# RMSNorm and matmul on one core: a load of eight tiles placed behind the stores of the first eight

## The chip, the cores and the metric

The kernel runs on one core of a Trainium2 chip. The metric is the device time of one execution in microseconds, as the median of several runs. The engines are named as in the profile: PE is the tensor engine, DVE the vector engine, ACT the scalar engine, POOL GpSimd, and SP (SyncE) the engine that issues nearly all transfers here.

## What is computed

```python
x: (16, 1024, 512) float32; gamma: (512,); weight: (512, 768) float32

rms = np.sqrt(np.mean(x ** 2, axis=-1, keepdims=True) + eps)
x_norm = x / rms * gamma
out = np.matmul(x_norm, weight)        # (16, 1024, 768) float32
```

There are 16,384 rows of x. The kernel works in 128 tiles of 128 rows: a tile of x has 262 KB, a tile of the output 393 KB. 33.6 MB of x and 1.6 MB of weights are read, and 50.3 MB are written.

## The kernel before

Tiles are handled in pairs (pair j is tiles 2j and 2j+1). For each pair GpSimd casts x to bf16, PE transposes it (two bf16 values as one float32 word) into PSUM, DVE evacuates the transposed pair, PE multiplies it with the weights (which hold gamma), and ACT and DVE scale one tile each by 1/rms on the way from PSUM to the output tile. ACT also sums the squares. The order on every engine is the order of the program.

x comes in groups of 16 tiles with two buffers, the output in groups of 8 tiles with three:

```python
XG, OG = 16, 8
AHEAD = 20
x_first, x_size = stretches(XG, {0: [2, 2, 4, 8], **{g: [8, 8] for g in (1, 4, 5, 6, 7)}})
o_first, o_size = stretches(OG, {0: [2, 2, 4], 1: [4, 4], last: [4, 4]})
...
xin = ctx.enter_context(tc.tile_pool(name="xin", bufs=2))
xbp = ctx.enter_context(tc.tile_pool(name="xb", bufs=4))
...
opsum = ctx.enter_context(tc.tile_pool(name="opsum", bufs=3, space=bass.MemoryType.PSUM))
outp = ctx.enter_context(tc.tile_pool(name="out", bufs=3))
```

So the first group is loaded in stretches of 2, 2, 4 and 8 tiles, the second in 8 and 8, the third and fourth in 16 at once. The first eight tiles are stored as 2, 2 and 4, the next eight as 4 and 4, then 8 at a time.

All loads of x and all stores are issued by SyncE, and SyncE takes its instructions in the order of the program: a store waits there until its tiles are scaled, and what stands behind it waits too.

```python
def load_until(i):
    while starts and starts[0] < i:
        load(starts.pop(0))          # one dma_start on SyncE for each stretch

def store(i):
    first, n = o_first[i], o_size[i]
    if i == first + n - 1:
        nc.sync.dma_start(out=rows(out, first, n), in_=held(o_tiles, OG, first, n))
```

Every group of 16 tiles but the first has four tiles (the last ones of the group, a quad) that PE doesn't transpose: GpSimd casts all four in one instruction, and DVE transposes them in 32x32 blocks, three instructions in each round of the loop.

```python
def cast_quad(q):
    quads[q] = quad_in.tile([P, 4, D], BF16, name="xq")
    nc.gpsimd.tensor_copy(out=quads[q], in_=held(x_tiles, XG, 4 * q, 4))
    ...

load_until(2)
load_weights(0)
load_weights(1)
load_until(2 * XG)                       # tiles 2 to 31
for _ in range(20):
    nc.sync.drain()
... # pair 0
for j in range(1, NP):
    load_until((2 * j + AHEAD + XG - 1) // XG * XG)
    if j + 3 < NP and quad_of(j + 3) is None:
        cast(2 * j + 6, nc.gpsimd, 2)
    if (2 * j + 2) % XG == 0 and 2 * j + 2 < NT:
        cast_quad((2 * j + 2 + XG - 4) // 4)
    elif 2 * j >= XG:
        move_quad(3)                     # 32x32 blocks of the quad, on DVE
    ...
    # the transposes of pair j + 2 are put between the matmuls of pair j
    for i, engine in ((2 * j, nc.scalar), (2 * j + 1, nc.vector)):
        a = accumulator()
        matmuls(i, a, range(K), feed)
        finish_tile(i, a, engine)        # scales, and stores when a stretch is full
```

`load_until` in the loop rounds up to whole groups: for j up to 6 it asks for tiles below 32, and from j = 7 for tiles below 48. `cast_quad` in round 7 casts tiles 28 to 31.

Of the kernel before, what the change touches and what calls it, by code (L numbers as in the profile page):

```python
# [18 lines left out]
def kernel(  # L19
# [18 lines left out]
    XG, OG = 16, 8  # L38
    AHEAD = 20
# [40 lines left out]
    def load(i):  # L80
        if i // XG not in x_tiles:
            x_tiles[i // XG] = xin.tile([P, XG, D], F32, name="xt")
        nc.sync.dma_start(out=held(x_tiles, XG, i, x_size[i]), in_=rows(x, i, x_size[i]))  # L83
# [3 lines left out]
    def load_until(i):  # L87
        while starts and starts[0] < i:
            load(starts.pop(0))

    def cast(i, engine, n=1):
        if i // 2 not in xb_tiles:
            xb_tiles[i // 2] = xbp.tile([P, 2, D], BF16, name="xb")
        engine.tensor_copy(out=xb_tiles[i // 2][:, i % 2:i % 2 + n, :], in_=held(x_tiles, XG, i, n))  # L94
# [13 lines left out]
    def norms(i, n):  # L108
        ssq = stats.tile([P, 4], F32, name="ssq")
        for t in range(n):  # L110
            square(i + t, ssq[:, t:t + 1])
        root(i, n, ssq)
# [30 lines left out]
    def transpose_tile(i):  # L143
        for h in range(2):
            transpose_word(i // 2, i % 2, h)
        evac(i // 2, i % 2, 1)
# [6 lines left out]
    def quad_of(j):  # L153
        return j // 2 if (2 * j) % XG >= XG - 4 and 2 * j >= XG else None
# [4 lines that stand above are left out]
        turned = quad_out.tile([P, 4, 2, P, 2], BF16, name="xTq")  # L159
        for n in range(2):  # L160
            xT_tiles[2 * q + n] = turned[:, 2 * n:2 * n + 2]
        words = quads.pop(q).rearrange("p t d -> p (t d)").bitcast(F32).rearrange("p (a w) -> p a w", w=P)
        out_words = turned.rearrange("p t h m c -> p (t h m c)").bitcast(F32).rearrange("p (a m) -> p a m", m=P)
        for tokens in range(0, P, B):
            for features in range(0, P, B):
                quad_moves.append((out_words[features:features + B, :, tokens:tokens + B],
                                   words[tokens:tokens + B, :, features:features + B]))

    def move_quad(n):
        for _ in range(min(n, len(quad_moves))):  # L170
            dst, src = quad_moves.pop(0)
            nc.vector.transpose(out=dst, in_=src)  # L172

    def scale(engine, dst, src, r):
        if engine is nc.scalar:
            nc.scalar.mul(out=dst, in_=src, mul=r)  # L176
        else:
            nc.vector.tensor_single_scalar(out=dst, in_=src, scalar=r, op=mybir.AluOpType.mult)  # L178

    def accumulator():  # L180
        return opsum.tile([P, 2, WIDE], F32, name="ops").rearrange("p a b -> p (a b)")
# [16 lines left out]
    def matmuls(i, acc, ks, feed=None):  # L198
        for k in ks:
            matmul(i, k, acc, 0, WIDE)  # L200
            if feed:
                feed()
            matmul(i, k, acc, WIDE, O)

    def finish_tile(i, acc, engine):
        scale(engine, out_tile(i), acc[:, :O], rstd_of[i])
        store(i)


    def feeder(pairs, gaps, alone=False):  # L210
        queue = [(j, t, h) for j in pairs for t in range(2) for h in range(2)]
        calls = iter(gaps)

        def feed():
            for _ in range(next(calls)):
                j, t, h = queue.pop(0)
                transpose_word(j, t, h)
                if alone and h == 1:
                    evac(j, t, 1)
                elif (t, h) == (1, 1):  # L220
                    evac(j)
        return feed

    with tc.manual_schedule():
        g_row = singles.tile([2, P, 2], F32)
        nc.scalar.dma_start(out=g_row, in_=gamma.rearrange("(h w c) -> h w c", w=P, c=2))
        nc.scalar.preload_act_table(AF.Sqrt)  # L227
        wv = weight.rearrange("(h w c) o -> w h (c o)", w=P, c=2)
        w_f32 = singles.tile([P, K, O], F32)

        def load_weights(h):
            nc.sync.dma_start(out=w_f32[:, 2 * h:2 * h + 2, :].rearrange("p c o -> p (c o)"), in_=wv[:, h, :])  # L232

        load_until(2)
        load_weights(0)
        load_weights(1)
        load_until(2 * XG)

        for _ in range(20):
            nc.sync.drain()  # L240


        warm = singles.tile([P, WIDE], BF16)
        nc.vector.memset(warm, 0.0)
        eps_sb = singles.tile([P, 1], F32)
        nc.vector.memset(eps_sb, float(eps))  # L246
        ident_f = singles.tile([P, P], F32)
        make_identity(nc, ident_f)
        spare = accumulator()

        def warm_up(n):
            for _ in range(n):
                nc.tensor.matmul(out=spare[:, :WIDE], lhsT=warm[:, :P], rhs=warm, start=True, stop=True)  # L253

        w_bf = singles.tile([P, K, O], BF16)

        def weights(k, engine, lo=0, hi=O):
            scale(engine, w_bf[:, k, lo:hi], w_f32[:, k, lo:hi], g_sb[:, k % 2, k // 2:k // 2 + 1])


        probe = singles.tile([16, 16 * 64], F32)

        def mark(counts):
            for k in counts:
                nc.sync.dma_start(out=probe[:k, 64 * k:64 * k + 4 * k], in_=x[:k, :4 * k])

        warm_up(6)
        gp = tpsum.tile([P, 2, 2], F32, name="tp")
        for c in range(2):
            nc.tensor.transpose(out=gp[:, c, :], in_=g_row[:, :, c], identity=ident_f[:2, :2])  # L270
        g_sb = singles.tile([P, 2, 2], F32)
        nc.vector.tensor_copy(out=g_sb, in_=gp)  # L272
        cast(0, nc.gpsimd)
        cast(1, nc.gpsimd)
        cast(2, nc.gpsimd, 2)
        norms(0, 2)
        warm_up(4)
        transpose_tile(0)
        transpose_tile(1)
        warm_up(2)  # L280
        weights(0, nc.vector, 0, WIDE)
        weights(0, nc.vector, WIDE, O)
        weights(1, nc.scalar)
        acc = [accumulator() for _ in range(2)]
        for i in range(2):
            matmuls(i, acc[i], [0, 1])
        weights(2, nc.vector)
        weights(3, nc.scalar)
        norms(2, 2)
        cast(4, nc.gpsimd)  # L290
        cast(5, nc.gpsimd)
        matmuls(0, acc[0], [2, 3])
        finish_tile(0, acc[0], nc.scalar)
        matmuls(1, acc[1], [2, 3], feeder([1], [2, 2], alone=True))
        finish_tile(1, acc[1], nc.vector)
        cast(6, nc.gpsimd, 2)

        mid, one, two, both = ([0, 0, 1, 1, 0, 1, 1, 0], [1, 1, 0, 1, 1, 0, 0, 0], [1, 0, 1, 0, 1, 0, 1, 0],
                               [1, 1, 1, 1, 1, 1, 1, 1])
        marks = {NP - 10: (12, 13, 14, 15)}  # L300
        for j in range(1, NP):
            load_until((2 * j + AHEAD + XG - 1) // XG * XG)
            if j + 3 < NP and quad_of(j + 3) is None:
                cast(2 * j + 6, nc.gpsimd, 2)
            if (2 * j + 2) % XG == 0 and 2 * j + 2 < NT:
                cast_quad((2 * j + 2 + XG - 4) // 4)
            elif 2 * j >= XG:
                move_quad(3)
            if j < 4:
                norms(2 * j + 2, 2)  # L310
            if 3 <= j < NP - 2:
                norms_by_four(j + 2)
            if j in marks:
                mark(marks[j])
            if j < 3:
                feed = feeder([j + 1], mid if j == 1 else one, alone=j == 1)
            elif j == 3:
                feed = feeder([4, 5], both)
            elif j + 2 < NP and quad_of(j + 2) is None:
                feed = feeder([j + 2], two)  # L320
            else:
                feed = None
# [3 lines that stand above are left out]
                finish_tile(i, a, engine)  # L326
# [35 lines left out]
```

## Time and profile before

| What | Before |
|---|---|
| time, median of 3 runs | 210.36 us (210.36 to 210.41) |
| span of the profiled execution | 209.0 us |
| granted clock of PE, mean | 0.983 of full speed |
| HBM read and written | 35.14 MB and 50.33 MB |

The profile is one execution, recorded by the hardware. Its page gives the busy time of each engine, the span in 40 slices (one digit for the busy share of an engine, numbers for GB/s), the chain of work that ended last, and groups of instructions. From the trace behind it one can ask for windows (busy time and number of instructions of PE, PE's weight loads, DVE, ACT and POOL, then granted clock, DMA share and GB/s of each stretch) and for timelines of one engine (start, duration, engine, line, what is written from what, number of instructions, and in brackets the idle time before and what ended it). A line such as L94 is a line of the kernel, which may be that of a helper: L94 is the cast of a pair, L158 the cast of a quad, L133 a transpose on PE, L140 its evacuation, L172 a 32x32 move on DVE, L194 a matmul, L176 and L178 the scaling on ACT and DVE, L83 a load of x, L191 a store.

### The profile page before, as it was taken

Reading aid. Unit: us, or ns where it says so; the run is one execution under the profiler, and the core shown is the slowest. Engines: PE = TensorE matmul, PEld = TensorE weight load, DVE = VectorE, ACT = ScalarE, POOL = GpSimd, SP = SyncE. Lnnn points to the kernel's source line nnn. Section 1 sums busy time; section 2 is a strip of 40 time slices with the busy share of each in tenths; the row PEclk is TensorE's granted clock in tenths of the full one; section 3 lists DMA queues with packets and bytes.
Section 4 is the critical chain, followed back from the end, with each engine's and each line's share of the span. In section 5 each row is a group of like instructions: output and inputs, shape, how many; then the busy total and the mean of one; then the engine's idle time right before and its main releaser. Section 6 shows DMA issues by size and latency. Waiting matters only on the chain.

```text
span 209.0 us, 3478 instructions
## 1 busy us (share of the span) xinstructions
PE 194.0 (93%) x1238; PEld 129.2 (62%) x1238; DVE 150.8 (72%) x270; ACT 149.4 (71%) x358; POOL 64.7 (31%) x65
## 2 busy tenths in 40 slices
PE   7699999999999999999999999999999999999700
PEld 2367776665677666666766667666677666666400
DVE  0465657997399957998499957998499957998300
ACT  4698787778677887788777887788777884976300
POOL 3247554003910292055210562025610365000000
PEclk9999999999999999999999999999999999999985
DMA  6999999999999999999999999999999999999991
GB/s 254 420 438 433 339 399 428 460 434 395 438 438 433 420 423 417 431 423 445 408 431 433 441 420 428 428 428 434 420 433 420 444 433 419 433 419 386 390 435 52
DMA packets 5601, 85.69 MB, mean 410 GB/s; under 512 B 718, under 2 KB 720, under 8 KB 1488
## 3 DMA queue, kind: packets, MB, share of 16 engines
q1 hardware_dynamic: 5580, 85.47, 96.9%
q8 instruction: 9, 0.15, 0.3%
q14 instruction: 8, 0.07, 0.1%
q10 hardware_dynamic: 4, 0.00, 0.0%
HBM read 35.14 MB, written 50.33 MB: 409 GB/s over the span
## 4 chain that ended last, share of the span: by engine, by line
PE 78%; DMA 14%; POOL 1%; DVE 1%; SPq 1%; issue 1%; POOLq 0%
PE ops L194 68%; DMA xt<-in_x_dram 14%; PE tp L133 9%; POOL xb L94 1%; DVE ot L178 1%; SPq L232 0%; SPq L83 0%; SPq L191 0%; POOLq L94 0%; DVE xT L140 0%
## 5 line engine op out<-in xcount | busy, mean ns | idle before, releaser
L194 PE MATMUL ops<-w_bf,xT 128*128 128x512 bf16 (+1 forms) x800 | 147.6, 326 | 0.9 <-DVE w_bf L178 0.8
L194 PEld LDWEIGHTS <-xT 128*128 128x128 bf16 x800 | 78.3, 98 | 46.8 <-issue 1.0
L176 ACT ACTIVATE ot<-ops,rstd 128x768 f32<-128x768 f32 x64 | 57.6, 901 | 41.9 <-PE ops L194 41.3
L94 POOL CAST xb<-xt 128x1024 bf16<-128x1024 f32 (+1 forms) x52 | 51.2, 1010 | 99.0 <-DMA xt<-in_x_dram 85.5
L98 ACT ACTIVATE jk<-xt 128x512 bf16<-128x512 f32 x128 | 78.8, 619 | 2.1 <-DMA xt<-in_x_dram 2.1
L178 DVE TENSOR_SCALAR ot<-ops,rstd 128x768 f32<-128x768 f32 x64 | 64.6, 1009 | 9.5 <-PE ops L194 9.0
L133 PE MATMUL tp<-ident_f,xb 128*128 128x128 f32 x200 | 54.1, 274 | 1.2 <-POOL xb L94 1.1
L140 DVE COPY xT<-tp 128x1024 bf16<-128x1024 bf16 (+1 forms) x53 | 34.6, 656 | 25.2 <-PE tp L133 24.6
L172 DVE STREAM_TRANSPOSE xTq<-xq 32x256 f32<-32x256 f32 x112 | 48.8, 435 | 1.9
L194 PE MATMUL ops<-w_bf,xTq 128*128 128x512 bf16 x224 | 42.8, 326 | 0.0
L133 PEld LDWEIGHTS tp<-ident_f,xb 128*128 128x128 f32 x200 | 27.9, 141 | 5.2 <-POOL xb L94 3.0
L194 PEld LDWEIGHTS <-xTq 128*128 128x128 bf16 x224 | 22.0, 98 | 12.3
L98 ACT ACTIVATION_READ_ACCUMULATOR jk<-xt 128x1 f32 x128 | 24.4, 191 | 0.0
L158 POOL CAST xq<-xt 128x2048 bf16<-128x2048 f32 x7 | 13.3, 1896 | 11.3 <-DMA xt<-in_x_dram 11.3
L102 ACT ACTIVATE rms<-ssq,eps_sb 128x4 f32<-128x4 f32 (+1 forms) x35 | 10.4, 297 | 1.1
L104 DVE RECIPROCAL rstd<-rms 128x4 f32<-128x4 f32 (+1 forms) x35 | 6.1, 175 | 6.3 <-ACT rms L102 5.6
L253 PE MATMUL ops<-warm 128*128 128x512 bf16 x12 | 4.4, 505 | 1.2 <-DVE eps_sb L246 1.2
L253 PEld LDWEIGHTS <-warm 128*128 128x128 bf16 x12 | 1.2, 117 | 2.6 <-DVE eps_sb L246 1.2
L176 ACT ACTIVATE w_bf<-w_f,g_sb 128x768 bf16<-128x768 f32 x2 | 1.9, 936 | 1.2 <-DMA w_f<-in_weight_dram 0.9
L272 DVE COPY g_sb<-tp 128x4 f32<-128x4 f32 x1 | 0.2, 161 | 3.2 <-PE tp L270 3.2
L227 ACT ACT_TABLE_LOAD x1 | 1.3, 1283 | 1.3 <-PEq L343 1.3
L178 DVE TENSOR_SCALAR w_bf<-w_f,g_sb 128x512 bf16<-128x512 f32 (+2 forms) x3 | 1.4, 481 | 0.6 <-DMA w_f<-in_weight_dram 0.6
(10 smaller groups left out, 1.9 us busy)
## 6 DMA issues: line engine op xcount, KB each, us to landing
out_dram<-ot SPq DMA_DIRECT2D x13, 3072.0 KB, 17.9
xt<-in_x_dram SPq DMA_DIRECT2D x11, 2048.0 KB, 18.3
xt<-in_x_dram SPq DMA_DIRECT2D x2, 4096.0 KB
out_dram<-ot SPq DMA_DIRECT2D x5, 1536.0 KB, 11.0
w_f<-in_weight_dram SPq DMA_DIRECT2D x2, 768.0 KB, 5.0
out_dram<-ot SPq DMA_DIRECT2D x2, 768.0 KB, 16.8
xt<-in_x_dram SPq DMA_DIRECT2D x2, 512.0 KB, 3.6
xt<-in_x_dram SPq DMA_DIRECT2D x1, 1024.0 KB
```

What stands on the lines that cost most here:

```text
L94: engine.tensor_copy(out=xb_tiles[i // 2][:, i % 2:i % 2 + n, :], in_=held(x_tiles, XG, i, n))
L98: nc.scalar.activation(out=jk, in_=held(x_tiles, XG, i)[:, 0, :], func=AF.Square, accum_out=ssq)
L102: nc.scalar.activation(out=rms[:, :n], in_=ssq[:, :n], func=AF.Sqrt, scale=1.0 / D, bias=eps_sb)
L104: nc.vector.reciprocal(out=rstd[:, :n], in_=rms[:, :n])
L133: nc.tensor.transpose(out=tp_tiles[j][:, t, h, :], in_=words[:, lo:lo + P], identity=ident_f)
L140: nc.vector.tensor_copy(out=dst[:, t:t + n, :], in_=src[:, t:t + n, :])
L158: nc.gpsimd.tensor_copy(out=quads[q], in_=held(x_tiles, XG, 4 * q, 4))
L172: nc.vector.transpose(out=dst, in_=src)
L176: nc.scalar.mul(out=dst, in_=src, mul=r)
L178: nc.vector.tensor_single_scalar(out=dst, in_=src, scalar=r, op=mybir.AluOpType.mult)
L194: nc.tensor.matmul(out=acc[:, lo:hi], lhsT=xT_tiles[i // 2][:, i % 2, k // 2, :, k % 2], rhs=w_bf[:, k, lo:hi], start=(k == 0), stop=(k == ...
L253: nc.tensor.matmul(out=spare[:, :WIDE], lhsT=warm[:, :P], rhs=warm, start=True, stop=True)
```

## The change

Tiles 24 to 31 are no longer loaded at the start, ahead of all stores. Their load is issued in round 4 of the loop, so on SyncE it stands behind the stores of tiles 0 to 7. It is meant to let the first stores run earlier, and to load tiles 24 to 31 nearer to their use. In round 4 `load_until` still asks for tiles below 32, and from round 7 on everything is as before.

```diff
         load_until(2)
         load_weights(0)
         load_weights(1)
-        load_until(2 * XG)
+        load_until(2 * XG - 8)
 ...
         for j in range(1, NP):
-            load_until((2 * j + AHEAD + XG - 1) // XG * XG)
+            if j >= 4:
+                load_until((2 * j + AHEAD + XG - 1) // XG * XG)
```

## The prediction

> **What bounds the kernel now.** I read the head of the page first, then the chain, then the last quarter, and then the stretch that the change touches.
>
> ```profile
> span 209.0 us, 3478 instructions
> PE 194.0 (93%) x1238; PEld 129.2 (62%) x1238; DVE 150.8 (72%) x270; ACT 149.4 (71%) x358; POOL 64.7 (31%) x65
> ...
> GB/s 254 420 438 433 339 399 428 460 434 395 438 438 433 420 423 417 431 423 445 408 431 433 441 420 428 428 428 434 420 433 420 444 433 419 433 419 386 390 435 52
> ...
> PE 78%; DMA 14%; POOL 1%; DVE 1%; SPq 1%; issue 1%; POOLq 0%
> ```
>
> Two things run nearly full: PE is busy 194.0 of 209.0 us, and the transfers move about 430 GB/s in nearly every slice. Which of them sets the end? The chain is 78% PE, and the largest other link in it is DMA. The end of the run, cut into windows (the last two columns are the DMA share and GB/s), tells which one has slack:
>
> ```profile
> 186.00:187.00 1.00, 1.00 (x9) 0.65 (x8) 0.96 (x3) 1.00 (x4) 0.00 (x0) 1.00 1.09 467
> 187.00:188.00 1.00, 1.00 (x8) 0.61 (x7) 0.97 (x2) 0.88 (x3) 0.00 (x0) 1.00 0.63 270
> 188.00:189.00 1.00, 1.00 (x8) 0.61 (x7) 0.96 (x3) 0.73 (x1) 0.00 (x0) 1.00 0.46 197
> 189.00:190.00 1.00, 1.00 (x8) 0.61 (x7) 0.95 (x4) 1.00 (x4) 0.00 (x0) 1.00 0.92 393
> ```
>
> From 187 to 189 the transfers run half empty while PE is full: the queue has nothing left and waits for PE to finish tiles 112 to 119, whose store goes out at 188.49. After it 16 tiles of output (6.3 MB, 14.6 us at 430 GB/s) remain. So the end follows PE: a microsecond lost on PE before 187 costs about a microsecond, and one of DMA alone is lost in that hole of about 1 us. Between 51.6 and 197 PE has no idle worth a name (5.00 of every 5 us, granted clock 1.00). Whatever the change does, it does before 52 us.
>
> There the page's slice at 21 to 26 us falls to 339 GB/s. In the windows:
>
> ```profile
> 22.00:23.00 1.00, 1.00 (x8) 0.75 (x7) 1.00 (x3) 0.63 (x3) 1.00 (x2) 1.00 1.05 410
> 23.00:24.00 1.00, 1.00 (x9) 0.70 (x7) 0.12 (x2) 0.95 (x2) 0.83 (x1) 1.00 1.24 360
> 24.00:25.00 1.00, 1.00 (x8) 0.66 (x7) 0.87 (x2) 1.00 (x4) 0.77 (x1) 1.00 0.90 229
> 25.00:26.00 1.00, 1.00 (x8) 0.74 (x7) 0.75 (x1) 0.17 (x2) 0.27 (x1) 1.00 0.80 197
> 26.00:27.00 1.00, 1.00 (x9) 0.69 (x8) 0.00 (x0) 0.92 (x2) 0.00 (x0) 1.00 0.80 281
> 27.00:28.00 1.00, 1.00 (x9) 0.70 (x7) 0.83 (x2) 1.00 (x3) 0.00 (x0) 1.00 0.96 403
> ```
>
> Against 430 these six windows lack 20 + 70 + 201 + 233 + 149 + 27 = 700 KB, or 1.6 us of transfer. The DMA share stays at 0.8 and above, so the queue isn't empty: the transfers in it are slow. By their order they are the load of tiles 24 to 31, the one that the change moves. The timeline of POOL (start, duration, line, count, idle before) shows what hangs on it:
>
> ```profile
> 24.23 1.04 POOL L94 CAST xb<-xt 128x1024 bf16<-128x1024 f32 x1 [0.40 <-PE tp L133]
> 28.64 1.90 POOL L158 CAST xq<-xt 128x2048 bf16<-128x2048 f32 x1 [3.36 <-DMA xt<-in_x_dram]
> 30.47 2.03 POOL L94 CAST xb<-xt 128x1024 bf16<-128x1024 f32 x2
> 33.34 1.04 POOL L94 CAST xb<-xt 128x1024 bf16<-128x1024 f32 x1 [0.84 <-PE tp L133]
> 50.52 3.01 POOL L94 CAST xb<-xt 128x1024 bf16<-128x1024 f32 x3 [16.13 <-DMA xt<-in_x_dram]
> ```
>
> The first reader of the moved load isn't tile 24 but the four-tile cast of tiles 28 to 31, which the loop asks for in round 7, ahead of the casts of pairs 11, 12 and 13. It starts at 28.64, having waited 3.36 us for the load. At 50.52 POOL gets tiles 32 to 47, and PE, which wants their transposes, has waited 0.41 us.
>
> **What the Trainium skill says.** "DMA: Bandwidth & Descriptors", section "Queues, rings and completion order": on each DMA engine a queue's descriptors are consumed in ring order. The trace agrees: the loads issued at 3.1 and 3.6 us land 13.6 and 18.0 us later, at 16.7 and 21.6, and a store issued at 12.98 takes 17.5 us to land because it stands behind them. So order of issue is order of service. The same page, "Anatomy of one DMA", says that a semaphore wait happens on the issuing sequencer and not in the DMA engines; in the trace SyncE's waits for the stores add up to 166 us, so a load behind a store is issued only when that store's tiles are done. "HBM Reference", Specifications, gives about 425 GB/s for a core that streams alone; the trace shows 420 to 440.
>
> **The change part by part.** Bytes, instructions and arithmetic stay the same; one 2.10 MB load changes its place.
>
> 1. *Ahead of the change.* Loads and weights up to tile 23 are issued as before, so PE's start and the casts up to pair 10 (24.23) stay. Cost 0.
>
> 2. *Stores 0 to 3* were issued at 12.98 and 16.1 and now are served directly after tile 23: 1.57 MB, 3.7 us, from 21.6 to 25.3. Nobody waits for them: three output tiles are there, so the first is wanted again only by tile 24. Gain 0.
>
> 3. *The issue of the load.* It follows the store of tiles 4 to 7, which goes out at 23.10 when pair 3 is done, so at about 23.5. Does the queue run dry? The first load is issued at 0.74, and 50 GB/s run in the window from 1 to 2 us and 308 in the next: some 1.3 us from issue to the first bytes. The store is then ready at 24.4, ahead of 25.3. No hole, with 0.9 us to spare. SyncE issues nothing later because of it: tiles 8 to 11 still go at 28.85.
>
> 4. *The landing of the load.* Ahead of it are now eight tiles of stores (3.15 MB) and it has itself 2.10 MB: 5.24 MB at 430 GB/s = 12.2 us after 21.6, so 33.8; POOL follows a landing after 0.2 (21.6 to 21.81). The cast of tiles 28 to 31 moves from 28.64 to about **34.0**, if the load runs at full rate, and to 35.6 if it is as slow as before.
>
> 5. *POOL behind it.* Cast 1.83 us from start to the next start (28.64 to 30.47), then 1.04 for pair 11: ready at 34.0 + 2.87 = 36.9 (before: 31.5). PE's first transpose of pair 11: evacuations follow every 3.04 us (DVE copies at 30.21, 33.24, 36.28), the one at 36.28 is pair 10's, and the next transpose on PE stands at 36.73. So 5.4 us of slack are used up nearly exactly: PE waits **about 0.2 us**; 1.7 us if the load stays slow. Pairs 12 and 13 follow 1.04 us apart while PE takes 3.04 a pair, so only one wait arises.
>
> 6. *DVE.* The 32x32 moves of tiles 28 to 31 stand in DVE's order at 34.77; now they wait for the cast's end, 34.0 + 1.9 = 35.9. DVE is 1.1 us late and can't catch up (4.8 of 5 us busy from 35 to 50). An accumulator of PE is wanted again two tiles, 3.04 us, after its own tile ends, and DVE's scaling takes 1.01 of that, so about 2 us are free, less where two tiles take only 2.6 us. The delay of 1.1 fits, barely. Cost 0, with a risk of some tenths.
>
> 7. *The load of tiles 32 to 47* has the same bytes ahead of it as before. It lands when it did (50.4), or up to 1.6 us earlier if the slow patch goes away; then PE's wait of 0.41 us vanishes. That is all that PE can win here.
>
> Sum, load at full rate: +0.2 - 0.4 = **-0.2 us**. Sum, load slow as before: +1.7, of which the wait at 51 us absorbs 0.4: **+1.3 us**.
>
> **Rivals.** (a) *Transfer bound:* the queue works better in the new order and the whole 1.6 us come off the end. The rates near 430 speak for it; against it, the dry queue at 187 to 189, where PE is the slower one. It would make 208.8. (b) *The cast takes over as the bound:* the load lands later than I sum, DVE and POOL both hold up PE, and two stalls add: the 5.4 us of slack have no reserve, each further microsecond of landing is a microsecond of stall. It would make 212 to 213. (c) *All hidden:* the slack holds and the wait at 51 us isn't there in executions without the slow patch: 210.4.
>
> **Range and chances.** Is the slow patch tied to this load's place, or to the moment? Loads of the same shape just before it run at 420 to 450 GB/s, so nothing in its form makes it slow; I give 60% that it doesn't come back. Then the time is 209.9 to 210.6, else 211 to 212. Weighted: 210.36 + 0.6 x (-0.2) + 0.4 x 1.3 = 210.8; the middle of the weight lies a little lower, so 210.6, with a range of 209.7 to 212.2. Two per cent are 4.2 us: to be faster by so much PE would have to lose idle time that it hasn't got; to be slower needs a load landing at about 39. Chances: 0.01, 0.95, 0.04.
>
> **What would show it.** Right: SyncE issues a load between the stores at 23.1 and 28.85; POOL's four-tile cast starts near 34 and names DMA as its releaser; the first stores land near 25; PE shows a short wait for POOL near 37 and none near 51; the end's hole at 187 to 189 is still there. Wrong: a cast that starts past 36, DVE waiting for POOL for more than 1.5 us with PE behind it, a queue that runs dry near 25 (step 3 has only 0.9 us), or another order of PE and DVE later on.

## The result and the profile after

The changed kernel takes 213.67 us (213.57 to 215.07, 6 runs), the kernel before 210.63 us in the same comparison (210.36 to 211.19, 6 runs). The ratio is 1.0154 with a 95% interval of 1.0125 to 1.0183: some 3.2 us slower, outside the predicted range of 209.7 to 212.2.

The page of the changed kernel (span, GB/s in 40 slices of 5.3 us, and the chain by engine):

```profile
span 211.9 us, 3454 instructions
...
GB/s 243 427 447 343 397 434 411 458 402 303 445 351 405 382 413 436 421 432 442 430 419 430 439 427 422 424 427 432 442 436 404 441 425 432 427 423 316 391 429 169
...
PE 82%; issue 8%; DMA 3%; POOL 2%; SPq 1%; DVE 0%; POOLq 0%
```

The weak slice is still there, one place sooner: 343 GB/s in the fourth slice (16 to 21 us) where the kernel before had 339 in the fifth. In windows (the last two columns are the DMA share and GB/s):

```profile
18.00:20.00 2.00, 2.00 (x16) 1.59 (x15) 1.50 (x3) 1.97 (x8) 2.00 (x3) 1.00 1.16 352
20.00:22.00 2.00, 1.95 (x15) 1.48 (x15) 0.95 (x2) 2.00 (x6) 0.91 (x1) 1.00 0.78 227
22.00:24.00 2.00, 2.00 (x14) 1.45 (x14) 1.12 (x3) 1.59 (x5) 0.97 (x1) 1.00 0.96 398
```

Against 430 they lack 156 + 406 + 64 = 626 KB, or 1.5 us. The slow stretch was 1.6 us before. But now it sits on the load of tiles 16 to 23: the load ahead of the first stores, whichever that is. It hits early work too: that load lands 19.2 us after its issue at 3.7, at 22.9 instead of 21.6.

POOL's timeline of the changed kernel shows what this made of the moved load:

```profile
23.03 3.01 POOL L94 CAST xb<-xt 128x1024 bf16<-128x1024 f32 x3 [2.12 <-PE ops L194]
37.35 1.89 POOL L158 CAST xq<-xt 128x2048 bf16<-128x2048 f32 x1 [11.31 <-DMA xt<-in_x_dram]
39.19 3.01 POOL L94 CAST xb<-xt 128x1024 bf16<-128x1024 f32 x3
50.70 3.01 POOL L94 CAST xb<-xt 128x1024 bf16<-128x1024 f32 x3 [8.50 <-PE tp L133]
```

The four-tile cast starts at 37.35 and not at 34.0, and pair 11 is ready at 40.2. PE's timeline (the bracket is idle time before, and what ended it):

```profile
36.08 0.81 PE L194 MATMUL ops<-w_bf,xT 128*128 128x256 bf16 x4
40.28 0.33 PE L133 MATMUL tp<-ident_f,xb 128*128 128x128 f32 x1 [3.40 <-POOL xb L94]
...
41.10 0.27 PE L133 MATMUL tp<-ident_f,xb 128*128 128x128 f32 x1
...
42.34 0.42 PE L133 MATMUL tp<-ident_f,xb 128*128 128x128 f32 x1
...
43.83 0.42 PE L133 MATMUL tp<-ident_f,xb 128*128 128x128 f32 x1
...
45.06 0.27 PE L133 MATMUL tp<-ident_f,xb 128*128 128x128 f32 x1
```

PE waits 3.40 us, and then there is a second loss that no wait shows. The transposes, 0.76 us apart otherwise, come 1.24, 1.49 and 1.23 us apart: 1.68 us more. In the windows from 42 to 44 the granted clock (the column ahead of the DMA share) is 0.50:

```profile
42.00:43.00 1.00, 1.00 (x5) 0.60 (x4) 0.95 (x3) 0.84 (x2) 0.20 (x1) 0.50 0.76 328
43.00:44.00 1.00, 1.00 (x4) 0.54 (x3) 0.67 (x2) 1.00 (x4) 0.00 (x0) 0.50 0.76 328
```

The kernel before has no wait near 37 us, but one of 0.41 us at 51 us, and SyncE issues a store at 82.40:

```profile
51.61 0.33 PE L133 MATMUL tp<-ident_f,xb 128*128 128x128 f32 x1 [0.41 <-POOL xb L94]
...
82.40 12.75 SPq L191 DMA_DIRECT2D out_dram<-ot  x2
```

The same store in the changed kernel:

```profile
87.06 12.75 SPq L191 DMA_DIRECT2D out_dram<-ot  x2
```

Sum on PE: 3.40 + 1.68, less the 0.41 of the old wait, which is gone: 4.67 us. The store goes out 4.66 us later. So PE's delay is accounted for, and it lasts unchanged to the last store (198.5 before, 203.1 after). But the spans differ by 2.9 us only: the end swallows some of it.

### The profile page after: what moved, and what is told of

Its sections match the earlier page's. It is cut to its first block, busy times and chain, and to the rows that moved or that the text cites. A ratio compares the mean times of both kernels' runs of the same rounds, so it can differ in the third digit from the quotient of the medians.

```text
span 211.9 us, 3454 instructions
## 1 busy us (share of the span) xinstructions
PE 195.5 (92%) x1214; PEld 130.7 (62%) x1238; DVE 151.1 (71%) x270; ACT 149.4 (71%) x358; POOL 64.7 (31%) x65
## 4 chain that ended last, share of the span: by engine, by line
PE 82%; issue 8%; DMA 3%; POOL 2%; SPq 1%; DVE 0%; POOLq 0%
PE ops L194 72%; PE tp L133 10%; DMA xt<-in_x_dram 3%; POOL xb L94 2%; DVE ot L178 0%; SPq L232 0%; SPq L83 0%; POOL xq L158 0%; POOLq L94 0%
## 5 line engine op out<-in xcount | busy, mean ns | idle before, releaser
L194 PE MATMUL ops<-w_bf,xT 128*128 128x256 bf16 (+1 forms) x783 | 148.2, 327 | 1.1 <-DVE w_bf L178 0.3
L194 PE MATMUL ops<-w_bf,xTq 128*128 128x256 bf16 (+1 forms) x217 | 42.4, 324 | 0.4
L133 PEld LDWEIGHTS tp<-ident_f,xb 128*128 128x128 f32 x200 | 28.6, 143 | 7.7 <-POOL xb L94 4.9
L158 POOL CAST xq<-xt 128x2048 bf16<-128x2048 f32 x7 | 13.3, 1895 | 19.2 <-DMA xt<-in_x_dram 19.2
L253 PE MATMUL ops<-warm 128*128 128x512 bf16 x12 | 5.5, 612 | 1.2 <-DVE eps_sb L246 1.2
```

Of the source, the lines that this page charges most:

```text
L133: nc.tensor.transpose(out=tp_tiles[j][:, t, h, :], in_=words[:, lo:lo + P], identity=ident_f)
L194: nc.tensor.matmul(out=acc[:, lo:hi], lhsT=xT_tiles[i // 2][:, i % 2, k // 2, :, k % 2], rhs=w_bf[:, k, lo:hi], start=(k == 0), stop=(k == ...
```

## The experiments

**Is it the order on GpSimd, or the order of the transfers?** First the transfers stay as in the changed kernel and the cast moves:

```diff
-            if (2 * j + 2) % XG == 0 and 2 * j + 2 < NT:
+            if j == 9:               # behind the casts of pairs 11 and 12
+                cast_quad(7)
+            elif j == 7:
+                pass
+            elif (2 * j + 2) % XG == 0 and 2 * j + 2 < NT:
                 cast_quad((2 * j + 2 + XG - 4) // 4)
             elif 2 * j >= XG:
-                move_quad(3)
+                move_quad(4 if j < 14 else 3)
```

> The changed kernel with one thing else: GpSimd casts tiles 28 to 31 in round 9, behind the casts of pairs 11 and 12, instead of in round 7 ahead of them, and DVE moves four blocks in a round instead of three. All transfers keep their order. Theory 1 (the late load holds the four-tile cast, GpSimd's order holds pair 11, PE starves for 3.4 us and then runs at a reduced clock): pair 11 is cast near 26, pair 12 near 37.4 to 38.4 and wanted at 39.8, PE's wait near 37 falls from 3.4 us to under 0.5 and the time to 210.4 to 211.2. Theory 2 (the new order of the transfers costs the time by itself, in slow stretches and in DMA engines that drift apart): the transfers are the same, so 213 to 214.

Measured: 210.70 us, ratio to before 1.0002 (0.9993 to 1.0011). The load comes about as late as in the changed kernel, but now it holds up only what needs it. POOL's timeline of this run:

```profile
36.94 1.04 POOL L94 CAST xb<-xt 128x1024 bf16<-128x1024 f32 x1 [8.83 <-DMA xt<-in_x_dram]
37.93 1.90 POOL L158 CAST xq<-xt 128x2048 bf16<-128x2048 f32 x1
```

Pair 12's cast waits for the load and still is in time; PE has no wait near 37. It has one of 1.72 us at 52.5, because DVE, with four moves a round, is behind with the quad; the granted clock stays at 1.00 after it. Counted from the first store, the store near 83 us is 1.3 us later than in the kernel before (70.68 us against 69.42), and at the end nothing of it is left. Theory 2 falls: the new order of the transfers costs no time by itself.

**The same loss without any change of transfers.** To the kernel before, matmuls of zeros are added ahead of tile 18, in an accumulator that the tile then overwrites. No work of the kernel is left out.

```diff
 a = accumulator()
+if i == 18:
+    for _ in range(24):          # 8 in the smaller run
+        nc.tensor.matmul(out=a[:, :WIDE], lhsT=warm[:, :P], rhs=warm, start=True, stop=True)
```

> The kernel before, all transfers in their old order, with 24 matmuls of zeros ahead of tile 18: PE is late by 24 x 0.215 = 5.2 us, less the 0.4 of its old wait at 51 us, so the stores of the middle are late by about 4.7, as in the changed kernel (4.66). If PE's delay alone makes the loss: 213.3 to 214.0, as the changed kernel. If the new order of the transfers has a part in it: nearer to 212 or below.

Measured: 213.88 us, ratio 1.0156 (1.0137 to 1.0175), against 1.0154 for the changed kernel. PE's delay suffices for the whole loss. The smaller dose:

> The kernel before with 8 matmuls of zeros (128x512, 0.22 us each, 1.7 us) ahead of tile 18: PE is late by 1.7 us from there on, with no idle time and no transfer changed. If the end follows PE one to one, as the prediction had it: 212.1. If one DMA engine that lags behind the others sets the end (after 204 us only 49 to 111 GB/s run in the kernel before), so that the end had some 1.7 us of slack against PE (4.66 us of delay at the last store, 2.9 at the end of the changed kernel): 210.4 to 210.8.

Measured: 210.92 us, ratio 1.0013 (0.9999 to 1.0027). Counted from the first store of each run, the store near 82 us is 1.2 us late (70.63 us against 69.42), and the end only 0.3: the prediction's sentence that a microsecond lost on PE costs about a microsecond fails here.

**How much of it is the clock?** In the changed kernel 16 such matmuls fill the time in which PE would wait.

> The changed kernel with 16 matmuls of zeros (128x512) put ahead of tile 18, so that PE works through the time in which it would wait for pair 11. If the drop of the granted clock to 0.66 between 40 and 45 us comes from PE's idle time and costs 1.3 us as I work out (4.66 us of delay in the stores at 82 us, less 3.4 us of wait, with 0.4 us of an old wait gone: 1.3 to 1.7), the clock stays at 1.00 and the stores of the middle move forward by 1.3 to 1.7 us; time 212.2 to 213, by how much of it the end takes over. If the clock falls for another reason, or costs nothing, 213.5 to 214.

Measured: 212.55 us, ratio 1.0093 (1.0069 to 1.0117), 1.1 us faster than the changed kernel. PE is never idle there, and the clock stays up, as the window after the filled wait shows:

```profile
40.00:45.00 5.00, 5.00 (x34) 3.55 (x34) 4.85 (x9) 2.79 (x7) 1.95 (x2) 1.00 0.99 426
```

Counted from the first store of each run, the store near 85 us is 1.5 us earlier than in the changed kernel (72.59 against 74.07), near the 1.68 us read off PE's timeline. So about a third of PE's delay is not the wait but the slow clock that follows it. The Trainium skill, "TensorE: Matmul & The Clock Gate" (Part 1: The HAM clock gate) says that the clock goes to half after an idle window of about 3.4 us; these runs agree as far as they go: 3.40 us idle brought 0.50, 1.72 us didn't.

**How far back may the load stand?**

```diff
-if j >= 4:
+if j >= 2:                       # behind the stores of tiles 0 to 3 only
     load_until(...)
```

> The load of tiles 24 to 31 behind the stores of tiles 0 to 3 only (round 2 instead of 4): 1.57 MB fewer ahead of it, 3.7 us. Theory 1: the cast of tiles 28 to 31 starts at 37.35 - 3.7 = 33.7, and the slack of pair 11 (36.7 - 2.9 = 33.8) just holds: PE's wait under 0.5 us, time 210.3 to 211.0. Theory 2 (putting a load behind stores costs by itself): 212 or more.

Measured: 210.89 us, ratio 1.0010 (1.0002 to 1.0019). POOL's four-tile cast:

```profile
33.33 1.90 POOL L158 CAST xq<-xt 128x2048 bf16<-128x2048 f32 x1 [7.64 <-DMA xt<-in_x_dram]
```

4.0 us sooner than behind eight tiles, and PE waits nowhere near 37. That fits the slack worked out in the prediction (a cast start at 33.8). Next, only the half of the load that nobody wants early moves:

```diff
-{0: [2, 2, 4, 8], **{g: [8, 8] for g in (1, 4, 5, 6, 7)}}
+{0: [2, 2, 4, 8], 1: [8, 4, 4], **{g: [8, 8] for g in (4, 5, 6, 7)}}
 ...
 load_until(2 * XG - 8)
+late = starts.pop(0)             # tiles 24 to 27: later, behind the stores
+load_until(2 * XG)               # tiles 28 to 31
+starts.insert(0, late)
```

> Tiles 28 to 31 are loaded ahead of all stores again, in a load of their own, and only tiles 24 to 27 behind the stores of tiles 0 to 7. Theory 1: the four-tile cast isn't late (near 25 to 27), pair 12 is wanted only at 39.8 and its load lands near 37 or sooner, so no wait of PE over 0.5 us; time 210.2 to 211. Theory 2: 213 or more, since a load still stands behind the stores and the slow stretch ahead of the first stores is still there.

Measured: 210.88 us, ratio 0.9999 (0.9988 to 1.0010). The quad's cast starts at 26.34, the cast of tiles 24 and 25 at 36.20, and PE waits for neither. It doesn't even have its old wait at 51 us, and the time is that of before: the 0.4 us that the prediction counted as the gain is worth nothing that shows at the end.

**What sets the end?** The hole at 187 to 189 us was read as a sign that the end follows PE. It can be filled:

```diff
-o_first, o_size = stretches(OG, {0: [2, 2, 4], 1: [4, 4], last: [4, 4]})
+o_first, o_size = stretches(OG, {0: [2, 2, 4], 1: [4, 4], last - 1: [4, 4], last: [4, 4]})
```

> The kernel before with the store of tiles 112 to 119 in two halves, so that the first half is issued some 5 us sooner and fills the hole at 187 to 189 us. If PE and the hole set the end: 1 to 1.7 us less, 208.7 to 209.4. If one lagging DMA engine sets it, which has no hole: within 0.4 us of before.

Measured: 210.78 us, ratio 1.0001 (0.9991 to 1.0011). The hole is gone (412 and 406 GB/s from 186 to 190), and the bulk of the transfers ends 1 us sooner. But a trickle follows it. Windows of this run:

```profile
203.00:204.00 1.00, 0.00 (x0) 0.00 (x0) 0.00 (x0) 0.00 (x0) 0.00 (x0) 0.50 0.30 123
204.00:205.00 1.00, 0.00 (x0) 0.00 (x0) 0.00 (x0) 0.00 (x0) 0.00 (x0) 0.50 0.14 61
206.00:207.00 1.00, 0.00 (x0) 0.00 (x0) 0.00 (x0) 0.00 (x0) 0.00 (x0) 0.50 0.12 49
```

and of the kernel before:

```profile
204.00:205.00 1.00, 0.00 (x0) 0.00 (x0) 0.00 (x0) 0.00 (x0) 0.00 (x0) 0.50 0.27 111
206.00:207.00 1.00, 0.00 (x0) 0.00 (x0) 0.00 (x0) 0.00 (x0) 0.00 (x0) 0.50 0.12 49
```

A full queue moves 430 GB/s with 16 DMA engines, 27 each, so 49 is, by this estimate, two engines that still work while fourteen have nothing left. The trace bears it out. It keeps 16 updates of the semaphore for each load of x and each store, taken here as one for each DMA engine's share. Of the last store before, fourteen shares land from 204.46 to 205.71, and two at 206.92 and 207.89. With the split store fourteen land by 205.00, and two at 207.52 and 207.57. So the end is that of the slowest DMA engines, and PE has some slack against them. From the runs: 1.2 us of delay of PE cost 0.3 (8 matmuls), 1.3 cost nothing (the cast moved), 3.2 cost 2.0 (the filled wait), 4.5 cost 3.3 (24 matmuls) and 4.7 cost 3.2 (the changed kernel). That is a slack of 1 to 1.5 us, and about one to one beyond it. The shares show where it goes: the first share of the changed kernel's last store lands 4.64 us later than before (209.10), as late as PE, and the last one only 2.92 us later (210.81), as the spans have it. The slowest engine is then 1.7 us behind the first, and no longer 3.4.

**Where does the slow stretch come from?** Two runs were meant to take the first stores out of the queue while tiles 24 to 31 are loaded. The first held them back in the program only:

> The kernel before with the stores of tiles 0 to 7 held back until the store of tiles 8 to 11 is issued (28.8 us), so that no store stands behind the load of tiles 24 to 31 while it runs. The slow stretch was 23 to 27 us in the kernel before, in the load of tiles 24 to 31, and 18.5 to 22 us in the changed one, in the load of tiles 16 to 23: in both the last load ahead of the first stores. If it comes from the stores that stand next in the queue, it is gone here: the load lands near 26.4 to 26.6 (21.5 + 4.9) and no window from 20 to 26 is under 400 GB/s. If it comes from the synchronous end of a long run of loads, or from the place of the data, it stays: landing near 28.5. The time itself isn't the point: the queue runs dry for some 2 us until 28.8.

Measured: 210.59 us, one run. SyncE's order of instructions came out as before, since nothing else is issued there in between: the first store went at 13.07. So it is a repeat of the kernel before, slow stretch included (246 and 296 GB/s from 24 to 28), and tells nothing of the question. The second put another store's wait ahead of them:

```diff
 if i == first + n - 1:
-    nc.sync.dma_start(out=rows(out, first, n), in_=held(o_tiles, OG, first, n))
+    held_back.insert(0, (first, n))
+    if i >= 11:                  # tiles 8 to 11 first, then 4 to 7, 2 to 3, 0 to 1
+        while held_back:
+            first, n = held_back.pop(0)
+            nc.sync.dma_start(...)
```

> The kernel before with the stores of tiles 0 to 7 issued behind the store of tiles 8 to 11, whose own wait (until 28.8 us) now stands ahead of them all: no store is in the queue while the load of tiles 24 to 31 runs. (The run named stores held was meant for this, but the order of SyncE's instructions came out as before.) If the slow stretch comes from the stores that stand next in the queue, it is gone: no window from 20 to 26 us under 400 GB/s, and the load lands at 26.4 to 26.8 instead of 28.5. If it comes from the end of the long run of loads, or from the data, it stays, and the landing is again near 28.5. The time: the queue is dry for 2 to 3 us until 28.8, in both cases; if the transfers' total counts, 211 to 213; if one lagging DMA engine sets the end and the dry stretch lets it catch up, 210 to 211.

Windows of this run, and its four-tile cast:

```profile
20.00:22.00 2.00, 1.95 (x15) 1.48 (x15) 1.02 (x2) 1.97 (x6) 1.10 (x2) 1.00 0.99 418
22.00:24.00 2.00, 2.00 (x16) 1.41 (x14) 0.99 (x3) 1.59 (x4) 1.60 (x3) 1.00 0.95 401
24.00:26.00 2.00, 2.00 (x15) 1.42 (x14) 1.30 (x2) 1.08 (x5) 0.83 (x1) 1.00 0.66 279
26.00:28.00 2.00, 2.00 (x15) 1.37 (x13) 1.28 (x2) 1.97 (x6) 0.47 (x1) 1.00 0.04 12
```

```profile
27.53 1.89 POOL L158 CAST xq<-xt 128x2048 bf16<-128x2048 f32 x1 [2.71 <-DMA xt<-in_x_dram]
```

The slow stretch is gone. From 24 us GB/s falls together with the share, since the queue runs out; before, the share stood at 0.8 to 0.9 with 197 to 281 GB/s. The cast starts 1.1 us sooner than before (28.64), less than the 1.6 summed in the prediction, because one part of the load came late (12 GB/s after 26): fifteen of the 16 shares land by 26.10 (before: 27.72), the last at 27.48 (before: 28.58). So stores that stand next in the queue slow the load ahead of them, in all 16 engines at once; by what means, no run here tells. The time of this run, 214.48 us, ratio 1.0185 (1.0168 to 1.0202), has the mechanism of the changed kernel at another place: the queue stands dry until the stores go at 28.4, the load of tiles 32 to 47 is issued at 31.61 instead of 29.28, behind all twelve tiles of stores, and PE waits 4.57 us for its casts at 55 us and then works at a clock of 0.50.

## Why the prediction was wrong

The direction of the chain was right: the moved load holds the four-tile cast, the cast holds pair 11 in GpSimd's order, and PE waits for pair 11. Steps 1 to 3 hold in what they cost: the casts of pairs 8 to 10 came up to 1.2 us later (23.03 instead of 21.81) but in time for PE, the stores of tiles 0 to 3 landed at 28.1 instead of 25.3 with nobody waiting, the load was issued at 23.48 as forecast, and the queue didn't run dry near 25 (449 GB/s from 24 to 26). Four terms were wrong.

- **Step 4, the landing: a cast start at 37.35 instead of 34.0.** "12.2 us after 21.6" had two faults. The slow stretch was counted as gone or as lying in the moved load; in fact it belongs to the load that stands ahead of the first stores, so it came back 5 us sooner, with 1.5 us. The rest, some 2 us, is a fault of the picture: a queue was treated as one pipe, with bytes divided by GB/s. What had been moved in the changed kernel from its start to 34.2 us, and to 37.35, when the cast begins:

```profile
DMA packets 1575, 13.11 MB, mean 383 GB/s; under 512 B 164, under 2 KB 166, under 8 KB 934
...
DMA packets 1696, 14.44 MB, mean 387 GB/s; under 512 B 178, under 2 KB 180, under 8 KB 948
```

  The load and everything ahead of it are 13.11 MB (7.86 up to tile 23, 3.15 of stores, 2.10 of its own). The 16 engines together had moved as much by 34.2, and yet the load is complete only at 37.3, when 14.44 MB have gone: the engines that are ahead were already 1.33 MB (3.1 us at 430 GB/s) into the next stores. In the kernel before, when tile 23 landed at 21.6, 8.34 MB had been moved for 7.86: 0.48 MB, 1.1 us. That is a spread larger by 2.0 us. The shares say who is late: of the moved load fifteen land from 34.33 to 35.16, up to 1.4 us behind the 33.8 of the prediction, and the last, alone, at 37.30. So the slow stretch, in all shares, and one late DMA engine make the 3.35 us, within the rounding. That the stores brought the spread isn't shown: a share comes late too in the run with no store in the queue (27.48). The Trainium skill, "DMA: Bandwidth & Descriptors" says (in "Two DMAs through the same engine are not ordered") that nothing orders transfers across the 16 engines; these landings agree.

- **Step 5, the wait on PE.** The slack was right but for a slip (5.2 us from 28.64 to 33.86, where the text has 5.4; the run behind four tiles shows a start at 33.33 without a wait), and with the true landing it would have given 37.35 + 2.87 - 36.73 = 3.5 us; measured 3.40. Missing was what a wait of that length does next: 1.68 us at half clock. Step 6 had DVE 1.1 us late. It waited 4.42 us for the cast, until 39.28, but no wait of PE came from that: PE went on at 40.28, just behind pair 11's cast, before DVE's next evacuation began at 40.74. With PE late by so much, the reserve that step 6 reckons with wasn't put to the test.

- **Step 7, the gain of 0.4 us.** The wait at 51 us did vanish, though only because PE was late by more; and 0.4 us of PE are worth nothing at the end (the run with tiles 28 to 31 ahead).

- **The bound.** "A microsecond lost on PE before 187 costs about a microsecond" is wrong for the first 1 to 1.5 us, and right beyond. The windows at 187 to 189 are a mean over 16 engines. Of the store that ends there twelve shares landed from 187.88 to 189.34, and four at 190.40, 191.12, 192.42 and 193.15: most engines had nothing left, and the slowest were up to 5 us behind. The half-empty windows were on the page, and so was the trickle behind 204 us; I read the first and not the second.

Put together: PE late by 3.40 + 1.68 - 0.41 = 4.67, less the slack of the end of 1 to 1.5, is 3.2 to 3.7; measured 3.0 between the medians, and 3.2 by the ratio. The rival that came nearest was (b), the cast as the bound at 212 to 213: its remark that each further microsecond of landing is a microsecond of stall is what happened, on a landing that was 3 us late, with the clock on top. Rival (a) is refuted by the result, and by the first run, in which the new order of the transfers saves nothing (210.70); but that transfers set the end was nearer to the truth than the prediction, only by single engines and not by the queue. Rival (c) is refuted by the result.

Nothing tried here beats the kernel before: the best runs equal it, and their last windows show the same trickle. Why single DMA engines fall behind stays open. The page of the kernel before has a candidate, in its list of queues:

```profile
q8 instruction: 9, 0.15, 0.3%
```

These are transfers of instructions of 16 KB, about 20 us apart. In all eleven traces the shares of every transfer land within 0.92 us of each other until the first of them, at 21.3 to 23.5 us, which takes 0.9 to 1.1 us; of the next transfer the last share comes 1.5 to 2.5 us after the first. The traces don't name the engine that moves it, and no run takes it away, so this isn't shown.

## What to carry to other kernels

When a transfer is moved back in a queue, look for its first reader in program order, not for the first reader by tile number: here a four-tile cast asked for the last tiles of a group ahead of the first ones. Reckon its landing by the slowest of the 16 DMA engines, with the spread that the trace shows (bytes moved at a landing, less bytes that stood up to it in the queue), and count an idle stretch of PE as long as this one (3.40 us) with the slow clock behind it. And before a microsecond of an engine is priced at the end, look at how the end itself looks: a few windows with some tens of GB/s after the last full one meant here that single DMA engines set it.

## What the runs showed of the hardware

- Loads ran at about half rate ahead of the first stores, if these already stood behind them in the queue (197 to 281 GB/s for 3 us, 1.5 to 1.6 us lost); with the stores issued later, the same load ran at 401 to 418 until the queue ran out. Where later loads meet stores in the kernel before, no window of 5 or 10 us between 30 and 185 is under 401 GB/s; the shares of one transfer are spread by then (over 2.6 us at 48 us), but that this is the reason is a guess.
- One DMA engine's share of a transfer came 0.9 us (before, at 28.58) to 2.1 us (changed, at 37.30) after the other fifteen; at 188 to 193 us the 16 shares of a store were spread over 5.3 us.
- After 3.40 us of idle time PE's clock didn't fall at once but about 1 us after work had begun again (1.00 from 40 to 41, 0.68 from 41 to 42, 0.50 until 44).
